# The denominators of a softmax, summed over the partitions from two exact 16-bit halves

## The chip, the cores and the metric

The kernel runs on one core of one Trainium2 chip. The metric is the time of one execution on the device in microseconds; of several executions the median is given. A profile is taken of one further execution. Engines are named as the profile names them: PE is TensorE's matmul, PEld its load of weights, DVE is VectorE, ACT is ScalarE, POOL is GpSimd, SP issues most DMAs.

## The reference

Two groups of tokens (256 of a context, 2048 of a sample grid) pass through two layers. Each layer normalizes its input, projects it, and mixes three branches: attention with 8 heads on 2 key-value heads of 64 columns, a short convolution, and pooling. The output projection adds the result to the input. What the change touches is the attention of the sample tokens, 2048 queries against 2048 + 256 keys:

```python
s = jnp.einsum('bqkgd,btkd->bkgqt', qblk, k).astype(jnp.float32) * scale
p = jax.nn.softmax(s, axis=-1)
return jnp.einsum('bkgqt,btkd->bqkgd', p.astype(v.dtype), v)
```

All inputs are 32-bit. The kernel keeps that precision by splitting numbers into a high and a low part and multiplying the parts.

## The kernel before

Each layer has two phases: one with the input projection and the other branches, and one with attention and the output projection (`phase_b`). The attention goes over four blocks of 512 queries, and in a block over the 8 heads (in the last block in another order, with head 3 last). The first block of a layer also holds the context's heads. A head has nine steps; a step does 256 keys:

- `qk` (L1191, L1192): TensorE makes the scores `st` of 256 keys x 512 queries, with keys on the partitions.
- `expo` (L1201, L1203): ScalarE takes the exponential twice, 32-bit as `P` and 16-bit as `ph`. GpSimd subtracts, `pl` = `P` - `ph` (helper `padd`, L181), also 16-bit. `ph` and `pl` are the two halves that TensorE multiplies with the values (`pv`, L1237 and L1244), three steps later. The `pl` of all nine steps are multiplied together behind the last `ph`.
- `zsum` (L1223, `Z`): VectorE sums `P` over the keys of three steps that share a partition, in three pieces, one piece in each of the next steps. GpSimd adds the tiles of the three groups of steps. The result is a tile `Z` of 128 x 512: for each query, 128 partial denominators.
- `max_pieces` (L1152, L1159, `mx`; L1153, L1161, `mr`): beside this, TensorE makes the scores of a later head once more, and VectorE takes their maximum. These `mx` tiles have two accumulators in PSUM, which rotate; other small groups, `lc` among them, take theirs from the same two.
- `outproj` (L1370 to L1372, `op`): the previous block's output projection, in small pieces between the steps.

The sum of `Z` over the partitions is `fin_b` (L1272, `lc`): for each of four groups of 128 queries, a matmul with the piece of `Z` as weights and a 128 x 2 tile of ones as the moving operand. VectorE takes the reciprocal `rl`. It is queued two steps after the step that issues the head's last `pv`, which is at the end of the next head's fifth step.

The last head of the last block is different: its `Z` isn't added, two tiles go into `lc`.

A manual schedule sets the order: each engine carries out its instructions in the order in which the code issues them, and semaphores hold an instruction back until what it reads is there and the buffer that it writes is free. Work is put into steps by tables (`todo`, `first`), and runs at the end or the start of its step.

The option that is changed was there before, switched off (`'fh': 0`).

Of the kernel before, what the change touches and what calls it, by code (L numbers as in the profile page):

```python
# [11 lines left out]
F16 = mybir.dt.float16  # L12
I32 = mybir.dt.int32
AF = mybir.ActivationFunctionType
ALU = mybir.AluOpType
# [16 lines left out]
PR = {'oa': 6, 'po': 4, 'q1': 3, 'q2': 5, 's0': 14, 's0p': 7, 'q1p': 2, 'ma': 3, 'mb': 1, 'd0': 3, 'd1': 2, 'dp': 1,  # L32
# [7 lines left out]
V_SCALE = 1.0  # L40

# [54 lines left out]
def hybrid_step(ctx: ExitStack, tc: tile.TileContext, A, O):  # L96
# [942 lines left out]
    def phase_b(l, xs_src, xp_src, xs_dst, xp_dst, nxt):  # L1039


        last = l == DEPTH - 1
        with ExitStack() as st, ExitStack() as left:
            def pool(name, bufs=1, side="right", to=st, **kw):
                return to.enter_context(tc.tile_pool(name=name, bufs=bufs, side=side, reuse_waits="tile", **kw))
# [44 lines left out]
            def make_unit(prompt, blk, h):  # L1090

                u = U()
                u.prompt, u.blk, u.h = prompt, blk, h
                u.t0 = blk * 512
                u.nst = 1 if prompt else 9
                u.KH, u.KL, u.V = kvs[prompt]
                u.g = h // 4
                u.pair = h // 2
                u.odd = h % 2
                u.last = prompt or u.odd  # L1100
                u.hi, u.lo = ((slice(64, 128), slice(0, 64)) if u.odd else (slice(0, 64), slice(64, 128)))
                u.fh = int(PR['fh'] and blk > 0)
                u.P, u.pp, u.low, u.z = {}, {}, [], []
                return u

# [152 lines left out]

            def split_z(u):
                z = u.z[0]  # L1260
                zh = wk.tile([128, 512], F16, tag="zh", name="zh", bufs=1)
                nc.scalar.copy(out=zh, in_=z)
                zl = wk.tile([128, 512], F16, tag="zl", name="zl", bufs=1)
                (padd if PR['ze'] else dsub)(zl, z, zh, ALU.subtract)
                u.z2 = (zh, zl)

            def fin_b(u, bc):
# [340 lines left out]
            def add_unit(prompt, blk, h, B):  # L1608
                u = make_unit(prompt, blk, h)
                u.B = B  # L1610
                u.S = len(steps)
                units.append(u)
                steps.extend((u, j) for j in range(u.nst))
# [36 lines left out]
            def do_pv(s):  # L1650
# [11 lines left out]
                if u.fh:  # L1662
                    at(s + d - min(PR['ds'], d - 1), lambda: split_z(u))
# [38 lines left out]
            wk = pool("b_wk")  # L1702
# [9 lines left out]
            for s in range(NSTEP + LAG + 16):  # L1712
# [44 lines left out]
                if cur:  # L1757
                    u, j = cur
# [64 lines left out]
```

## Time and profile before

| what | value |
|---|---|
| median of three executions | 3217.0 us (3216.62 to 3223.13) |
| profiled execution | 3230.8 us, span 3229.0 us |
| PE, PEld busy | 3077.7 us (95%), 2443.4 us (76%) |
| DVE, ACT, POOL busy | 2320.5 us (72%), 1833.1 us (57%), 2017.3 us (62%) |
| attention, blocks 2 to 4 of layer 1 | from about 994 to 1600 us |
| the same of layer 2 | from about 2563 to 3172 us |
| mean granted clock of TensorE | 0.982 |

The span goes from the first to the last instruction; the rest of the time lies around it. Matmuls are pipelined, and a record is longer than what it adds: the distance from one start to the next is what counts. The granted clock is a share of 2.4 GHz; 0.50 is the 1.2 GHz level.

### The profile page before, as it was taken

The page shows a single profiled execution, that of the slowest core. Times are in us where ns is not written, and L with a number is a line of the kernel's source. Part 1 is how long each engine was busy: PE and PEld are TensorE (multiplying, and loading weights), DVE is VectorE, ACT ScalarE, POOL GpSimd, SP SyncE. Part 2 cuts the span into 40 slices and gives each one's busy share as a digit, 9 for nine tenths or more (in the row PEclk, how much of TensorE's full clock was granted, in tenths as well). Part 3 has the DMA queues.
Part 4 walks back from the last instruction along what each step waited for, and adds up shares of the span by engine and source line. Part 5 has one row for each costly group of instructions (what it writes and reads, how often), then busy time and mean ns, then how long its engine had stood idle before and what let it go on. Part 6 is the DMA issues. An engine that isn't in the chain of part 4 may idle for free. (4 is left out here: it accounts for less than half of the span.)

```text
span 3229.0 us, 48081 instructions
## 1 busy us (share of the span) xinstructions
PE 3077.7 (95%) x17642; PEld 2443.4 (76%) x17642; DVE 2320.5 (72%) x3728; ACT 1833.1 (57%) x2634; POOL 2017.3 (62%) x1290
## 2 busy tenths in 40 slices
PE   7899999999999999999979899999999999999997
PEld 5788888776677777777769788987676777677775
DVE  5655576358888888888757545843778888888886
ACT  3323233237777777777742323331668887787785
POOL 2424363226888888888833334621578888898885
PEclk9999999999999999999989999999999999999999
DMA  7245744346233241323433455434623432242444
GB/s 248 75 143 164 241 158 149 118 130 167 77 120 113 68 125 58 105 79 110 137 127 100 152 160 193 132 98 120 175 66 119 130 97 80 86 131 86 131 144 149
DMA packets 371970, 408.40 MB, mean 126 GB/s; under 512 B 33428, under 2 KB 319640, under 8 KB 370968
## 3 DMA queue, kind: packets, MB, share of 16 engines
q1 hardware_dynamic: 371736, 405.33, 40.6%
q8 instruction: 140, 2.29, 0.3%
q14 instruction: 94, 0.77, 0.1%
HBM read 285.69 MB, written 119.55 MB: 126 GB/s over the span
## 5 line engine op out<-in xcount | busy, mean ns | idle before, releaser
L181 POOL TENSOR_TENSOR pl<-P,ph 128x1024 f16<-128x1024 f32 (+2 forms) x594 | 1235.7, 2091 | 282.7 <-ACT ph L1203 260.9
L1153 DVE TENSOR_REDUCE mr<-mx 128x1 f32<-128x512 f32 x1024 | 696.3, 685 | 276.8 <-PE mx L1152 270.8
L1201 ACT ACTIVATE P<-st 128x1024 f32<-128x1024 f32 x576 | 636.1, 1104 | 286.3 <-PE st L1192 281.2
L1223 DVE TENSOR_REDUCE Z<-P 128x152 f32<-128x912 f32 (+2 forms) x576 | 695.9, 1209 | 6.6 <-ACT P L1201 5.5
L1203 ACT ACTIVATE ph<-st 128x1024 f16<-128x1024 f32 x584 | 591.6, 1013 | 0.0
L1152 PE MATMUL mx<-KH,T 128*128 128x512 f32 x1024 | 485.4, 475 | 33.5 <-DVE mr L1153 16.7
L639 PE MATMUL rest<-xh,wh 128*128 128x512 f32 (+1 forms) x1264 | 477.8, 378 | 0.7 <-ACT wh L426 0.7
L641 PE MATMUL rest<-xh,wl 128*128 128x512 f32 (+1 forms) x1264 | 468.8, 371 | 2.0 <-DVE wl L428 2.0
L640 PE MATMUL rest<-xl,wh 128*128 128x512 f32 (+1 forms) x1264 | 469.2, 371 | 0.0
L1191 PE MATMUL st<-T,KH 128*128 128x512 f32 x1152 | 462.3, 401 | 3.1 <-ACT ph L1203 3.1
L1192 PE MATMUL st<-T,KL 65*128 65x512 f32 x1152 | 460.1, 399 | 0.0
L1237 PE MATMUL pv<-ph,V 128*128 128x512 f16 x1152 | 351.8, 387 | 2.2 <-ACT P L1201 1.8
L1152 PEld LDWEIGHTS mx<-KH,T 128*128 128x128 f32 x1024 | 194.2, 190 | 192.7 <-DVE mr L1153 83.0
L428 POOL TENSOR_TENSOR wl<-wf,wh 128x512 fp32r<-128x512 f32 x88 | 124.1, 1410 | 244.5 <-ACT wh L426 226.4
L639 PEld LDWEIGHTS rest<-xh,wh 128*128 128x128 f32 x1264 | 240.7, 190 | 44.4 <-issue 5.5
L641 PEld LDWEIGHTS rest<-xh,wl 128*128 128x128 f32 x1264 | 240.1, 190 | 43.8 <-DVE wl L428 2.6
L640 PEld LDWEIGHTS rest<-xl,wh 128*128 128x128 f32 x1264 | 240.6, 190 | 36.9
L1192 PEld LDWEIGHTS st<-T,KL 65*128 65x128 f32 x1152 | 219.2, 190 | 47.7
L1191 PEld LDWEIGHTS st<-T,KH 128*128 128x128 f32 x1152 | 220.0, 191 | 42.5 <-ACT ph L1203 6.1
L480 PE MATMUL qkv<-wl,xh 128*128 128x256 f32 x864 | 247.5, 287 | 4.7 <-DVE wl L428 3.1
L479 PE MATMUL qkv<-wh,xh 128*128 128x256 f32 x864 | 251.3, 291 | 0.0
L481 PE MATMUL qkv<-wh,xl 128*128 128x256 f32 x864 | 246.9, 286 | 0.0
(234 smaller groups left out, 5559.8 us busy)
## 6 DMA issues: line engine op xcount, KB each, us to landing
wo<-woH SPq DMA_DIRECT2D x144, 256.0 KB
wo<-woL SPq DMA_DIRECT2D x144, 256.0 KB
wf<-in_w_in SPq DMA_DIRECT2D x50, 512.0 KB
wa<-in_w_ada SPq DMA_DIRECT2D x24, 1024.0 KB
wf<-in_w_in SPq DMA_DIRECT2D x19, 1024.0 KB
woH<-wgh SPq DMA_DIRECT2D x64, 256.0 KB
woL<-wgl SPq DMA_DIRECT2D x64, 256.0 KB
T<-qH SPq DMA_DIRECT2D x128, 128.0 KB
```

Of the source, the lines that this page charges most:

```text
L181: nc.gpsimd.tensor_tensor(out=out, in0=a, in1=b, op=op)
L639: nc.tensor.matmul(out=ps[:, 0:b.n], lhsT=wh[:, k, ms], rhs=b.h[:, k, :], start=(k == 0), stop=False)
L640: nc.tensor.matmul(out=ps[:, 0:b.n], lhsT=wh[:, k, ms], rhs=b.l[:, k, :], start=False, stop=False)
L641: nc.tensor.matmul(out=ps[:, 0:b.n], lhsT=wl[:, k, ms], rhs=b.h[:, k, :], start=False, stop=(k == KD - 1))
L1152: nc.tensor.matmul(out=ps, lhsT=u.T1[:, q * 128:(q + 1) * 128], rhs=u.KH[u.g][:, c * 512:(c + 1) * 512])
L1153: nc.vector.reduce_max(out=mr[:, q, c:c + 1], in_=ps, axis=AX.X)
L1191: nc.tensor.matmul(out=ps[:, i, :], lhsT=u.KH[u.g][:, kt], rhs=u.T1, start=True, stop=False)
L1192: nc.tensor.matmul(out=ps[:, i, :], lhsT=u.KL[u.g][0:65, kt], rhs=u.T2, start=False, stop=True)
L1201: nc.scalar.activation(out=P, in_=ps, func=AF.Exp, scale=0.125)
L1203: nc.scalar.activation(out=ph, in_=ps, func=AF.Exp, scale=0.125)
L1223: nc.vector.tensor_reduce(out=z[:, c], in_=u.P[grp][:, 0:ns, c, :].rearrange("p s n t -> p n s t"), axis=AX.XY, op=ALU.add)
L1237: nc.tensor.matmul(out=u.po, lhsT=u.V[u.g][:, 2 * j + i, :], rhs=ph[:, i, :], start=(j == 0 and i == 0), stop=False)
```

## The change

For the heads of the second to fourth block (all but the last head of the last block), `split_z` makes two 16-bit tiles of `Z`: `zh`, the rounded value, and `zl` = `Z` - `zh`. Both lie in one tile `zhl`, which takes a buffer of the tag `Z` (three of 2 KB, as before). ScalarE makes `zh`; `zl` is GpSimd's in the first layer and VectorE's in the second. `lc` then takes eight 16-bit matmuls with 16-bit ones in place of four 32-bit ones, each of which is two passes in the trace. `split_z` is queued at the end of the step before `lc`.

```diff
-      'n2': 4, 'fh': 0, 'tpos': 0, 'ze': 0, 'ds': 1, 'zb': 3, 'dl': 2, 'm3': 1000, 'hk': 2, 'hc': 2,
+      'n2': 4, 'fh': 1, 'tpos': 0, 'ze': 0, 'ds': 1, 'zb': 3, 'dl': 2, 'm3': 1000, 'hk': 2, 'hc': 2,
...
-                u.fh = int(PR['fh'] and blk > 0)
+                u.fh = int(PR['fh'] and blk > 0 and not (blk == 3 and h == 3))
...
             def split_z(u):
                 z = u.z[0]
-                zh = wk.tile([128, 512], F16, tag="zh", name="zh", bufs=1)
+                two = wk.tile([128, 2, 512], F16, tag="Z", name="zhl", bufs=PR['zb'])
+                zh, zl = two[:, 0], two[:, 1]
                 nc.scalar.copy(out=zh, in_=z)
-                zl = wk.tile([128, 512], F16, tag="zl", name="zl", bufs=1)
-                (padd if PR['ze'] else dsub)(zl, z, zh, ALU.subtract)
+                (dsub if last else padd)(zl, z, zh, ALU.subtract)
                 u.z2 = (zh, zl)
```

TensorE, first layer, second block, at the fifth step of a head (`zhl` is the tile of both halves; what an instruction waits for stands in brackets). Before:

```order
L1192 MATMUL st<-T_9655,KL 128x512
L1191 MATMUL st<-T_9262,KH 128x512
L1192 MATMUL st<-T_9655,KL 128x512
L1159 MATMUL mx<-KH,T_9544 128x256 x2
L1272 MATMUL lc<-vones,Z 128x2 x4
```

With the change:

```order
L1159 MATMUL mx<-KH,T_10152 128x256 [waits DVE_49]
L1159 MATMUL mx<-KH,T_10152 128x256
L1272 LDWEIGHTS zhl [waits Activation_49]
L1272 MATMUL lc<-vones_h,zhl 128x2 [waits DVE_49]
L1272 LDWEIGHTS zhl [waits Pool_49]
L1272 MATMUL lc<-vones_h,zhl 128x2
```

The place is the same; six more pairs like the last follow. The second load, the first of `zl`, waits for GpSimd, where the old group waited for GpSimd's addition of `Z`.

GpSimd, first layer, around the same place, with the change (before, the row with `zhl` isn't there and nothing else differs):

```order
L181 TENSOR_TENSOR Z<-Z 128x512 [waits DVE_49,PE_49,Pool_49]
L181 TENSOR_TENSOR pl<-P,ph 128x1024 [waits PE_49,Activation_49]
L181 TENSOR_TENSOR pl<-P,ph 128x1024 [waits Activation_49]
L181 TENSOR_TENSOR zhl<-Z,zhl 128x512 [waits Activation_49]
L181 TENSOR_TENSOR pl<-P,ph 128x1024 [waits PE_49,Activation_49] x4
```

The subtraction stands behind the two `pl` that follow the addition of `Z`.

VectorE, second layer, with the change:

```order
L1153 TENSOR_REDUCE mr<-mx 128x1 [waits PE_49]
L184 TENSOR_TENSOR zhl<-Z,zhl 128x512 [waits Activation_49]
L1161 TENSOR_REDUCE mr<-mx 128x2 [waits PE_49]
L1223 TENSOR_REDUCE Z<-P 128x190
L1161 TENSOR_REDUCE mr<-mx 128x2 [waits PE_49]
L1275 RECIPROCAL rl<-lc 128x4 [waits PE_49]
```

The subtraction is new; the two `mr` behind it free the accumulators that `lc` and the next `mx` take.

## Rows read from the trace of the kernel before

**Rows 1.** The page, part 1: busy time, share of the span, instructions.

```profile
PE 3077.7 (95%) x17642; PEld 2443.4 (76%) x17642; DVE 2320.5 (72%) x3728; ACT 1833.1 (57%) x2634; POOL 2017.3 (62%) x1290
```

**Rows 2.** Windows: length; PE, PEld, DVE, ACT, POOL busy; clock, DMA share, GB/s.

```profile
994.00:1600.00 606.00, 598.54 (x3446) 454.44 (x3446) 509.53 (x707) 458.82 (x562) 508.57 (x270) 1.00 0.30 89
2563.00:3172.00 609.00, 598.96 (x3415) 450.90 (x3414) 509.04 (x710) 487.34 (x671) 534.14 (x323) 1.00 0.35 107
```

**Rows 3.** Groups by line and shape: busy us, mean ns of one, idle before.

```profile
L1272 PE MATMUL lc<-vones,Z 128*128 128x2 f32 x592 | 74.6, 248 | 5.1 <-DVE mr L1153 2.6 <-DVE mr L1161 1.4 <-POOL pl L181 0.2
L1272 PEld LDWEIGHTS lc<-vones,Z 128*128 128x128 f32 x592 | 73.1, 193 | 14.0 <-DVE mr L1153 5.3 <-issue 4.8 <-POOL pl L181 2.1
L1237 PEld LDWEIGHTS <-V 128*128 128x128 f16 x1152 | 68.2, 99 | 57.5 <-issue 35.6 <-PE mx L1152 2.5
...
L181 POOL TENSOR_TENSOR pl<-P,ph 128x512 f16<-128x512 f32 x18 | 21.2, 1179 | 0.0
L1304 ACT CAST mixh<-o 128x512 fp32r<-128x512 f32 x32 | 19.9, 621 | 22.8 <-POOL o L181 16.3 <-DVE o L184 6.4
...
L184 DVE TENSOR_TENSOR o<-o,zs 128x512 f32<-128x512 f32 x2 | 1.4, 692 | 0.1
```

**Rows 4.** Timeline of PE at one head: start, us, instruction, idle before.

```profile
1076.35 1.01 PE L1272 MATMUL lc<-vones,Z 128*128 128x2 f32 x8
```

**Rows 5.** Timeline of POOL at the same head.

```profile
1076.21 2.16 POOL L181 TENSOR_TENSOR pl<-P,ph 128x1024 f16<-128x1024 f32 x1
```

**Rows 6.** Timelines of PE and POOL at the first and the last of 22 heads.

```profile
994.04 0.24 PE L1272 MATMUL lc<-vones,Z 128*128 128x2 f32 x1 [0.19 <-DVE mr L1161]
994.81 2.16 POOL L181 TENSOR_TENSOR pl<-P,ph 128x1024 f16<-128x1024 f32 x1
...
1570.94 0.24 PE L1272 MATMUL lc<-vones,Z 128*128 128x2 f32 x1
1570.79 2.16 POOL L181 TENSOR_TENSOR pl<-P,ph 128x1024 f16<-128x1024 f32 x1
```

**Rows 7.** Timelines of DVE and POOL in the first layer's projection phase.

```profile
372.97 1.79 DVE L784 TENSOR_TENSOR wg<-wo,gate 128x512 f32<-128x512 f32 x1
372.93 1.29 POOL L428 TENSOR_TENSOR wl<-wf,wh 128x512 fp32r<-128x512 f32 x1 [0.60 <-ACT wh L426]
```

**Rows 8.** Timelines of ACT, POOL, DVE and PE at a head of the second layer.

```profile
2755.23 1.00 ACT L1203 ACTIVATE ph<-st 128x1024 f16<-128x1024 f32 x1
2755.27 2.16 POOL L181 TENSOR_TENSOR pl<-P,ph 128x1024 f16<-128x1024 f32 x1
2756.70 0.68 DVE L1161 TENSOR_REDUCE mr<-mx 128x2 f32<-128x512 f32 x1
2758.55 0.68 DVE L1161 TENSOR_REDUCE mr<-mx 128x2 f32<-128x512 f32 x1
2757.54 1.02 PE L1272 MATMUL lc<-vones,Z 128*128 128x2 f32 x8
2759.47 0.58 PE L1152 MATMUL mx<-KH,T 128*128 128x512 f32 x1
```

**Rows 9.** The same at a head with a late `ph`.

```profile
3119.38 0.99 ACT L1203 ACTIVATE ph<-st 128x1024 f16<-128x1024 f32 x1
3120.45 2.14 POOL L181 TENSOR_TENSOR pl<-P,ph 128x1024 f16<-128x1024 f32 x1 [0.49 <-ACT ph L1203]
3120.24 0.35 PE L1272 MATMUL lc<-vones,Z 128*128 128x2 f32 x2
```

**Rows 10.** Windows around two stops of PE, columns as in group 2.

```profile
472.84:475.77 2.93, 0.00 (x1) 0.00 (x1) 2.90 (x9) 1.29 (x3) 0.82 (x1) 0.88 0.01 3
475.10:481.90 6.80, 6.13 (x28) 6.13 (x29) 6.53 (x15) 0.00 (x0) 5.24 (x4) 0.50 0.39 117
2241.85:2244.13 2.28, 0.00 (x1) 0.03 (x1) 0.00 (x0) 0.00 (x0) 0.00 (x0) 1.00 1.10 241
2244.13:2251.00 6.87, 6.87 (x30) 5.56 (x31) 4.84 (x7) 0.60 (x1) 0.00 (x0) 1.00 1.11 216
```

## The prediction

> **What bounds the kernel now.** I read the page first, then the windows of the two attention stretches, then the timeline around one group of matmuls, engine by engine. The page says TensorE: busy 95% of the span, every other engine at most 72% [rows 1]. The windows of the three changed blocks say it more sharply [rows 2]: 598.54 of 606 us in the first layer and 598.96 of 609 us in the second. So in these stretches a microsecond that TensorE waits is a microsecond of the result, and one that it saves is saved, unless another engine then ends last. GpSimd is the next busiest, 508.57 and 534.14 us of them; most of that is `pl`, 2.16 us a step. VectorE has 509 us.
>
> The place that the change touches is the group `lc` at the end of the fifth step of the next head, once for each head. TensorE takes its instructions in order: what stands behind a late `lc` (the output projection, `pv`, the next `mx` and `st`) is late too, and ScalarE, VectorE and GpSimd wait for `st`.
>
> **The change, part by part.** 46 heads are changed: 23 of 24 in each layer.
>
> *Removed.* Today's `lc` group is eight passes over 32-bit weights: 1.01 us of records, each some 0.25 long, so starts 0.11 apart and 0.88 us of TensorE [rows 3, 4]. *Put in its place* are eight passes over 16-bit weights. No such small 16-bit pass is in the trace. Bounds: as dear as now (no gain), or nearly free (0.8 us saved). The nearest row is the 16-bit load of `V`, 99 ns of record against 193 for the load in `lc` [rows 3], about half; by it a pass takes about 0.055 and a group saves 0.45 us: 23 x 0.45 = 10 us in each layer. [...] I keep the row.
>
> *Added, ScalarE.* The copy `zh`, bounded by a cast of the same 128x512 size: 0.62 us [rows 3]. It stands behind `ph`, in time in which ScalarE waits for the next `st`, and costs nothing by itself. The tile is taken from the three buffers of `Z`; I find no reduce that waits longer for that, since what it takes over was read a step or more earlier.
>
> *Added, GpSimd, first layer.* The subtraction `zl`: 1.18 us by the `pl` of 128x512 [rows 3]. It stands on GpSimd's queue behind the addition of `Z` and two `pl`, and `lc` needs it one step later. Before, `lc` needed only that addition. In the head that I took as the example, `lc` starts at 1076.35 [rows 4], while the second of the two `pl` runs from 1076.21 for 2.16 us, to 1078.37 [rows 5]. `zl` is then done at 1079.55. The first pass (on `zh`) can run, the second load waits: it would have started at 1076.46, so TensorE stands for 3.1 us. The backlog doesn't come from a full queue that a shift would change: the addition of `Z` waits for a reduction on VectorE that follows the end of the head's `pv`, and both `pl` stand behind it. The same two rows for each head give `pl` ending after `lc` starts by 2.93 us in the first head [rows 6], 2.01 in the last of them, 1.3 to 3.8 in the 22 heads, on average 2.06; the 23rd has it done in time. The stall is thus 2.06 + 1.18 - 0.11 = 3.1 us, 22 x 3.1 = 69 us (hand-overs left out), less the 10 us of shorter passes: +59 us. Nothing gives it back: while TensorE stands, the others run dry and wait for the next `st`.
>
> *Added, VectorE, second layer.* There the subtraction is VectorE's, between the last `mr` of a step and the first of the next. Undisturbed it takes 0.69 us (a subtraction or product of 128x512 from SBUF: 692 ns [rows 3]). But both inputs lie in SBUF, and such an operation waits out a running GpSimd operation: a product of the same size took 1.79 us and ended 0.54 us after the GpSimd subtraction that ran beside it (372.97 + 1.79 = 374.76, and 372.93 + 1.29 = 374.22) [rows 7]. In the attention stretch GpSimd runs a `pl` most of the time. Example [rows 8]: `ph` ends at 2756.23, `zh` at 2756.85; a `pl` runs to 2757.43, so `zl` ends at about 2757.97 (not 2757.54). The first `mr` behind it then ends at 2758.65 instead of 2757.38, 1.27 us late. `lc` takes the accumulator that this `mr` frees, so it starts at 2758.65 instead of 2757.54; and the second `mr`, also 1.27 late (2760.50), holds the next `mx`, which stood at 2759.47: TensorE is 1.03 us late behind it, with the shorter passes already used up. In the worst heads `ph` itself is late: ending at 3120.37, with a `pl` from 3120.45 to 3122.59 [rows 9], `zl` ends at 3123.13, the `mr` at 3123.81, and `lc` at 3120.24 is 3.6 us late. The same arithmetic over the 22 heads before the last ones gives 0.4 to 3.5 us each, 36 us in all: +36 us. Without the wait for GpSimd it would be about 18 us; with it I have only the rows of another phase, so 18 to 36 is the bound, and I take 36 since `pl` reads and writes SBUF just as that subtraction did.
>
> *The clock.* A TensorE that stands some 3 us can lose its clock. It stood 2.93 us, and the next 6.80 us were granted 0.50, the 1.2 GHz level [rows 10]; it stood 2.28 us at another place and kept 1.00. 6.8 us at half clock cost 3.4 us of work. For the 22 stalls of the first layer that is 0 to 75 us. Theirs, some 2.9 us after the first pass, lie at the longer of the two, but two cases of another phase are few; I take one stall in four: +19 us.
>
> **Sum.** 59 + 36 + 19 = 114 us. The rows come from an execution of 3230.8 us (span 3229.0, 1.8 around it), which is 13.8 us (0.4%) over the median of 3217.0; the terms are differences, so I set them on the median: 3217 + 114 = 3331, say 3330 us.
>
> **The rivals.**
> - *The clock holds.* For it: the 2.28 us that cost nothing [rows 10]. Then 3217 + 59 + 36 = 3312.
> - *The clock falls after nearly every stall.* For it: the 2.93 us [rows 10]. 3217 + 95 + 75 = 3387. The Trainium skill's page "TensorE: Matmul & The Clock Gate", section "Why this matters for your kernels", speaks for this one: it warns of idle gaps between bursts of matmuls because the clock goes to half behind them.
> - *VectorE is hardly held by GpSimd, and passes are nearly free.* 3217 + 69 - 23 x 0.8 + 16 = 3284. For it: no row has these two instructions side by side.
> - *The subtraction is in time (the other side).* If GpSimd were as far as `lc` with its queue, the place of the wait would be empty, only the shorter passes would count, 46 x 0.45 = 21 us: 3196. It decides at `zl` ending before `lc` starts, that is GpSimd 3.1 us further than the rows have it [rows 4 to 6]. One head of 23 is that far. In the second layer, `zl` would have to leave the `mr` behind it on time, and 0.69 us alone doesn't.
> - *No change that shows.* The stalls would have to shrink to the 21 us saved; half of the first layer's alone is more.
>
> **How the numbers follow.** Stalls with some falls of the clock (3315 to 3370), the forecast: 0.45. Stalls without (3290 to 3315): 0.22. Clock falling nearly always (3370 to 3400): 0.09. Small waits (3255 to 3290): 0.15. In time: 0.05; no change: 0.04. The range 3270 to 3390 leaves out about 2 in 10. Its ends are worked from the bounds: below, 69 - 18 + 16 with a seventh off the stalls, and no fall of the clock; above, all 22 falls. Faster by over 0.2% (about what a measurement of this kernel can tell from no change): 0.05; within: 0.04; slower: 0.91.
>
> **What would show it.** In the first layer, `lc` waiting for GpSimd's `zl` some 3 us in 22 heads, and `zl` starting when the second `pl` ends, 1.2 us long. In the second, `zl` on VectorE taking 0.7 us where no `pl` runs and up to 2.3 where one does, `lc` waiting for VectorE's `mr`, a stretch of 609 us becoming about 645. 16-bit `lc` loads of about 0.1 us of record. The first layer's stretch of 606 us becoming 665 to 740. Wrong it is if `lc` waits under 1 us for `zl` in the first layer, if the `op` behind `lc` comes no later after the step's `st` than now, or if the granted clock of the first stretch falls well under 0.9.

## The result, and the profile after

The kernel with the change takes 3368.25 us (median), the kernel before 3216.81 on the same chip: the ratio is 1.0459 (95% interval 1.044 to 1.0479), so it is slower by some 148 to 151 us. Forecast were 3330 us in a range of 3270 to 3390, that is +113.

The first part of the page (busy time, share of the span, instructions) and the row of granted clocks, with the change:

```profile
PE 3102.8 (92%) x17642; PEld 2450.3 (73%) x17642; DVE 2366.0 (70%) x3751; ACT 1856.7 (55%) x2680; POOL 2051.2 (61%) x1313
...
PEclk9999999999999989989989999999999999999999
```

Against [rows 1] the matmuls are as many, but TensorE is busy 92% of the span where it was 95%, and 25 us longer in all, though the new passes are shorter: part of its work ran at a lower clock.

Windows from the first changed `lc` to the last in each layer, with the change (columns as in group 2):

```profile
991.94:1690.40 698.46, 624.63 (x3443) 470.24 (x3442) 513.49 (x707) 470.57 (x583) 531.43 (x292) 0.93 0.26 78
2650.80:3316.45 665.65, 610.57 (x3442) 453.21 (x3442) 550.03 (x735) 498.62 (x696) 545.02 (x327) 0.96 0.31 96
```

And the same stretches, between the same two instructions, of the kernel before:

```profile
994.04:1599.70 605.66, 598.24 (x3442) 454.11 (x3443) 509.19 (x707) 458.69 (x561) 508.38 (x270) 1.00 0.30 89
2563.92:3177.12 613.20, 602.74 (x3442) 454.57 (x3443) 511.45 (x713) 489.44 (x677) 538.34 (x328) 1.00 0.34 105
```

The first layer loses 92.8 us and the second 52.5. Together that is 145.3, a little more than the 139.2 between the two profiled executions (3369.97 and 3230.8 us). In both layers the granted clock is down. A mean of 0.93 over 698 us is some 98 us at 0.50 (0.07 x 698 / 0.5); 0.96 over 666 us is some 53.

What the new instructions cost (view of the tile `zhl` with the change; the three numbers are shortest, median and longest in ns):

```profile
L1272 PEld LDWEIGHTS <-zhl x368: 95/96/119, 991.7 to 3316.6; 128*128 128x128 f16 x184
L1272 PE MATMUL lc<-vones_h,zhl x368: 163/163/188, 991.9 to 3316.6; 128*128 128x2 f16 x184
L1263 ACT CAST zhl<-Z x46: 602/619/656, 990.8 to 3314.4; 128x512 f16<-128x512 f32 x46
L181 POOL TENSOR_TENSOR zhl<-Z,zhl x23: 1141/1151/1185, 994.9 to 1690.5; 128x512 f16<-128x512 f32 x23
L184 DVE TENSOR_TENSOR zhl<-Z,zhl x23: 794/1203/7153, 2648.4 to 3315.0; 128x512 f16<-128x512 f32 x23
```

And what TensorE waited for at `lc` (view of the tile `lc`: us, times):

```profile
  POOL zhl L181: 68.4, 23
  PE lc L1272: 44.4, 24
  DVE mr L1161: 37.3, 14
  DVE mr L1153: 7.9, 14
  ACT P L1201: 7.4, 8
```

The prices of ScalarE and GpSimd are those of [rows 3]. GpSimd's 23 subtractions hold TensorE for 68.4 us. In the second layer the same engine waits at `lc` for `mr` (37.3 us), and for ScalarE's `P` by the record (7.4); the 7.9 us of the other `mr` were there before (2.6 and 5.3 us in [rows 3]). The 44.4 us named "PE lc" are VectorE's `rl`, which waits for `lc`, not TensorE.

A head of the first layer with the change (timeline: start, us, engine, instruction, idle before):

```profile
1051.15 1.29 POOL L181 TENSOR_TENSOR Z<-Z 128x512 f32<-128x512 f32 x1 [0.35 <-DVE Z L1223]
1052.40 4.28 POOL L181 TENSOR_TENSOR pl<-P,ph 128x1024 f16<-128x1024 f32 x2
1056.62 1.17 POOL L181 TENSOR_TENSOR zhl<-Z,zhl 128x512 f16<-128x512 f32 x1
...
1053.53 0.61 ACT L1263 CAST zhl<-Z 128x512 f16<-128x512 f32 x1
...
1054.77 0.16 PE L1272 MATMUL lc<-vones_h,zhl 128*128 128x2 f16 x1
1057.85 0.35 PE L1272 MATMUL lc<-vones_h,zhl 128*128 128x2 f16 x7 [2.92 <-POOL zhl L181]
1058.05 0.56 PE L1370 MATMUL op<-wo,ch 128*128 128x256 f32 x1
1058.41 0.41 PE L1371 MATMUL op<-wo,ch 128*128 128x256 f32 x1
```

`zh` is done at 1054.14, before `lc` starts; the first pass runs at 1054.77. GpSimd still has a `pl` until 1056.68 and only then begins `zl`. TensorE stands for 2.92 us, and the `op` behind `lc` (L1371) takes 0.41 us where such a record takes 0.28 at full clock (below, at 2741.40). The clock around this stop, in windows:

```profile
1054.93:1057.85 2.92, 0.01 (x1) 0.01 (x1) 1.63 (x2) 1.70 (x2) 2.92 (x3) 0.85 0.99 297
1057.00:1063.80 6.80, 5.96 (x26) 4.93 (x27) 2.64 (x5) 1.07 (x2) 2.88 (x2) 0.50 0.34 90
```

The 6.80 us at 0.50, 1.2 GHz, begin 0.85 us before the stop ends; TensorE works for 5.96 us of them. In the trace 20 of the first layer's 22 stops have a fall to 0.50, which begins between 2.4 us before the stop's end and 1.1 us behind it.

Two heads of the second layer with the change, one with a short and one with a long subtraction:

```profile
2739.54 0.79 DVE L184 TENSOR_TENSOR zhl<-Z,zhl 128x512 f16<-128x512 f32 x1 [0.40 <-ACT zhl L1263]
2740.26 0.68 DVE L1161 TENSOR_REDUCE mr<-mx 128x2 f32<-128x512 f32 x1
...
2740.99 0.34 PE L1272 MATMUL lc<-vones_h,zhl 128*128 128x2 f16 x8 [0.94 <-ACT P L1201]
2741.19 0.37 PE L1370 MATMUL op<-wo,mixh 128*128 128x256 f32 x1
2741.40 0.28 PE L1371 MATMUL op<-wo,mixh 128*128 128x256 f32 x1
...
2742.84 0.50 PE L1152 MATMUL mx<-KH,T 128*128 128x512 f32 x1 [0.24 <-DVE mr L1161]
...
2947.07 2.15 POOL L181 TENSOR_TENSOR pl<-P,ph 128x1024 f16<-128x1024 f32 x1
2949.18 1.26 POOL L181 TENSOR_TENSOR oy<-oy,fg 128x512 f32<-128x512 f32 x1
2950.40 4.16 POOL L181 TENSOR_TENSOR pl<-P,ph 128x1024 f16<-128x1024 f32 x2
...
2947.96 7.15 DVE L184 TENSOR_TENSOR zhl<-Z,zhl 128x512 f16<-128x512 f32 x1 [0.38 <-ACT zhl L1263]
2955.03 0.68 DVE L1161 TENSOR_REDUCE mr<-mx 128x2 f32<-128x512 f32 x1
2955.77 0.35 PE L1272 MATMUL lc<-vones_h,zhl 128*128 128x2 f16 x8 [7.14 <-DVE mr L1161]
2956.34 0.41 PE L1371 MATMUL op<-wo,mixh 128*128 128x256 f32 x1
```

In the first head `lc` starts when the `mr` behind `zl` ends (2740.94), 0.94 us late; the record names ScalarE's `P` there, but VectorE's `mr` ends last. In the second head `zl` starts under a running `pl` and ends at 2955.11, 0.55 us after the fourth GpSimd instruction (2954.56). `lc` stands 7.14 us, and the `op` behind it runs at half clock (0.41 us). The row of eight passes also prices a pass: (0.34 - 0.16) / 7 = 26 ns apart, where the 32-bit ones were 0.11 us apart; the `op` starts 0.20 us after the group. A group saves 0.88 - 0.21 = 0.67 us, 15 us in each layer.

### The profile page after: what moved, and what is told of

Its sections match the earlier page's. It is cut to its first block, busy times and chain, and to the rows that moved or that the text cites. A ratio compares the mean times of both kernels' runs of the same rounds, so it can differ in the third digit from the quotient of the medians.

```text
span 3368.2 us, 48107 instructions
## 1 busy us (share of the span) xinstructions
PE 3102.8 (92%) x17642; PEld 2450.3 (73%) x17642; DVE 2366.0 (70%) x3751; ACT 1856.7 (55%) x2680; POOL 2051.2 (61%) x1313
## 4 chain that ended last, share of the span: by engine, by line
PE 57%; DVE 15%; POOL 6%; issue 4%; ACT 4%; DMA 3%; SPq 1%; POOLq 0%; DVEq 0%; ACTq 0%
PE mx L1152 6%; PE rest L639 5%; PE rest L640 5%; PE rest L641 5%; PE pv L1237 5%; PE st L1191 5%; PE st L1192 5%; DVE Z L1223 4%; DVE mr L1153 4%; PE pv L1244 4%; POOL pl L181 3%; PE op L1370 2%; PE op L1371 2%; PE op L1372 2%; PE qkv L480 1%
## 5 line engine op out<-in xcount | busy, mean ns | idle before, releaser
L1152 PE MATMUL mx<-KH,T 128*128 128x512 f32 x1024 | 499.6, 489 | 35.4 <-DVE mr L1153 16.8
L1191 PE MATMUL st<-T,KH 128*128 128x512 f32 x1152 | 473.3, 411 | 3.3 <-ACT ph L1203 3.3
L1192 PE MATMUL st<-T,KL 65*128 65x512 f32 x1152 | 469.4, 407 | 0.0
L1237 PE MATMUL pv<-ph,V 128*128 128x512 f16 x1152 | 364.7, 400 | 2.2 <-ACT P L1201 1.8
L1152 PEld LDWEIGHTS mx<-KH,T 128*128 128x128 f32 x1024 | 201.4, 197 | 204.9 <-DVE mr L1153 82.9
L639 PEld LDWEIGHTS rest<-xh,wh 128*128 128x128 f32 x1264 | 240.8, 191 | 44.4 <-issue 5.5
L1192 PEld LDWEIGHTS st<-T,KL 65*128 65x128 f32 x1152 | 226.0, 196 | 50.4
L1191 PEld LDWEIGHTS st<-T,KH 128*128 128x128 f32 x1152 | 227.6, 198 | 45.8 <-ACT ph L1203 6.8
```

The lines of the kernel that those rows point to most:

```text
L639: nc.tensor.matmul(out=ps[:, 0:b.n], lhsT=wh[:, k, ms], rhs=b.h[:, k, :], start=(k == 0), stop=False)
L1152: nc.tensor.matmul(out=ps, lhsT=u.T1[:, q * 128:(q + 1) * 128], rhs=u.KH[u.g][:, c * 512:(c + 1) * 512])
L1191: nc.tensor.matmul(out=ps[:, i, :], lhsT=u.KH[u.g][:, kt], rhs=u.T1, start=True, stop=False)
L1192: nc.tensor.matmul(out=ps[:, i, :], lhsT=u.KL[u.g][0:65, kt], rhs=u.T2, start=False, stop=True)
L1237: nc.tensor.matmul(out=u.po, lhsT=u.V[u.g][:, 2 * j + i, :], rhs=ph[:, i, :], start=(j == 0 and i == 0), stop=False)
```

## The experiments

All edits are to the changed kernel; the stretches are those of the windows above, first layer / second layer (before: 605.7 / 613.2 us; with the change 698.5 / 665.7). A ratio is to the kernel before on the same chip: 3226.36 us for experiments 1 to 4, 3222.98 for 5 to 8, 3220.26 for 9 to 12. The expected times are set on 3217 us, so a few microseconds between them and a measured time say little. A stretch is of one execution.

**1. The first layer alone.** Does each layer carry its own loss?

```diff
-                u.fh = int(PR['fh'] and blk > 0 and not (blk == 3 and h == 3))
+                u.fh = int(PR['fh'] and blk > 0 and not last and not (blk == 3 and h == 3))
```

> The split in the first layer alone. If the two layers lose apart from each other, this run keeps the first layer's loss of the changed kernel (its stretch from the first to the last changed lc is 698 us against 606, so +93) and gives back the second's (666 against 613, +52): about 3310 us. If what is lost in the first layer is partly regained later, less than 3300.

Measured: 3310.12 us, ratio 1.0259 (1.0244 to 1.0274); stretches 697.7 / 612.8. The layers are independent: the first keeps all its loss, the second has none.

**2. `lc` without the low half.** `zl` is still made, on the same engines in the same place, but nothing reads it: `lc` takes `zh` twice, so its passes are as many.

```diff
-                u.z2 = (zh, zl)
+                u.z2 = (zh, zh)
```

> zl is made by the same engines at the same places, but lc takes zh twice, so the low half is left out of the sum. Theory of the wait: in the first layer nothing reads zl, TensorE's 68 us of waiting and the clock's falls go, and the shorter passes gain some 15 us: its stretch is about 590 us. In the second layer lc is held by the mr behind zl on VectorE and not by zl, so its stretch stays near 660. Total about 3217 - 15 + 50 = 3250. Rival, the added work itself (GpSimd's and ScalarE's queues longer): the first stretch stays over 650 and the total over 3300. If in the second layer too it is the wait for zl itself that counts, total about 3190.

Measured: 3265.51 us, ratio 1.0127 (1.0108 to 1.0145). Its windows:

```profile
986.14:1585.46 599.32, 588.70 (x3443) 438.06 (x3442) 508.67 (x707) 470.39 (x583) 532.51 (x292) 1.00 0.30 91
2545.38:3210.82 665.44, 610.51 (x3443) 453.02 (x3442) 550.00 (x735) 498.77 (x696) 544.82 (x327) 0.96 0.31 96
```

In the first layer the whole loss is gone, and the clock is 1.00 again, though the stretch gains 6 us and not the 15 that the shorter passes were to bring: the loss was TensorE's wait for `zl` with what hangs on it; the copy, the subtraction and the shared buffer of `Z` cost nothing there. The second layer stays as it was, to 0.2 us: there `lc` isn't late by its own operand, but by the `mr` that stands behind `zl` on VectorE.

**3. The clock kept up.** 22 matmuls of 256 columns whose result nobody reads run ahead of each first-layer `lc`, in its wait. What the first layer regains is the clock's share, as far as the added matmuls fit into the wait.

```diff
-                ps = pmx.tile([128, 4, 2], F32, tag="mx", name="lc")
+                full = pmx.tile([128, 512], F32, tag="mx", name="lc")
+                ps = full[:, 0:8].rearrange("p (q e) -> p q e", e=2)
+                for _ in range(22 if u.fh and not last else 0):
+                    nc.tensor.matmul(out=full[:, 256:512], lhsT=ones_r, rhs=u.KH[u.g][:, 0:256])
```

> As the changed kernel, but in the first layer 22 matmuls of 256 columns that nobody reads stand ahead of each lc group, some 2.6 us of the 3.0 us that TensorE waits there. If the clock's falls cost what the half-clock stretches of the first layer say (20 falls, 99 us at half, so 40 to 49 us), the clock stays at 1.00 and the time falls to 3325 to 3335 although TensorE has more to do. Rival, the falls cost nothing beside the waits: 3365 to 3375.

Measured: 3332.53 us, ratio 1.0322 (1.0305 to 1.034). Its first window:

```profile
980.39:1643.52 663.13, 645.80 (x3927) 499.64 (x3928) 511.32 (x707) 470.14 (x583) 533.91 (x293) 1.00 0.27 82
```

With 484 matmuls more the stretch is 35.3 us shorter than 698.46, at a clock of 1.00. So some 35 us of the first layer's 93 are the clock, and 57 the waits less the shorter passes. (TensorE's busy time says the same: 624.63 with the change, 588.70 in experiment 2, a difference of 35.9.) The ratios put what the added matmuls give back higher, 1.0459 to 1.0322, 44 us with 36 to 53 as its interval; either way it is some two fifths to half of the layer's loss.

**4 and 5. The other engine.** The subtraction on VectorE in both layers, or on GpSimd in both.

```diff
-                (dsub if last else padd)(zl, z, zh, ALU.subtract)
+                dsub(zl, z, zh, ALU.subtract)
```

> The subtraction on VectorE in both layers. If VectorE's way costs in the first layer what it costs in the second (+52 rather than +93): about 3325. If GpSimd's queue is not what makes zl late, no change from 3368. If VectorE's waiting for GpSimd's pl is worse in the first layer: over 3368.

```diff
-                (dsub if last else padd)(zl, z, zh, ALU.subtract)
+                padd(zl, z, zh, ALU.subtract)
```

> The changed kernel with GpSimd subtracting in both layers, lc where it is. If the second layer's queue of GpSimd stands at lc as the first's does (the second pl ends 2.0 us behind the start of lc in most heads there too), its loss becomes that of the first, 90 to 100 rather than 52: about 3410. If VectorE is the worse place, under 3368.

Measured: on VectorE 3306.21 us, ratio 1.0248 (1.0223 to 1.0273), stretches 641.7 / 670.6; on GpSimd 3415.66 us, ratio 1.0598 (1.0569 to 1.0627), stretches 702.2 / 716.8. VectorE's way costs +36 us in the first layer (less than the 52 expected), GpSimd's +104 in the second. The two mechanisms belong to the engines, not to the layers. What TensorE waits for at `lc` with GpSimd in both:

```profile
  POOL zhl L181: 142.2, 45
```

That is 3.2 us each, where the first layer with the change has 3.0.

**6 to 8. `lc` two steps later.** Then GpSimd has the time it lacks. First the division of the change, then GpSimd in both layers, then a control without the split.

```diff
-                d = PR['dp'] if u.prompt else PR['dl'] if u is units[-1] else PR['d1' if u.blk else 'd0']
+                d = PR['dp'] if u.prompt else PR['dl'] if u is units[-1] else PR['d1' if u.blk else 'd0'] + 2 * (u.blk > 0)
...
-                    at(s + d - min(PR['ds'], d - 1), lambda: split_z(u))
+                    at(s + d - min(PR['ds'] + 2, d - 1), lambda: split_z(u))
```

> lc and all that follows from it two steps (some 5.3 us) later, the split where it is; GpSimd subtracts in the first layer, VectorE in the second. Theory of the wait: zl is 3.1 us late, so two steps later it is there, the first layer loses nothing and gains its 15 us. In the second layer VectorE still stands for GpSimd's pl ahead of two mr, but lc is no longer near: a part of the 52 us stays, 15 to 40. Total 3217 - 15 + 25 = 3227, 3215 to 3245. Rival, the engines' added work: 3300 or more.

The second has `padd(zl, ...)` of experiment 5 besides:

> The same with GpSimd subtracting in both layers, so VectorE gets no new work. Theory of the wait: both layers lose nothing and gain 0.65 us in each of 46 heads, 30 us: 3187, 3185 to 3205, faster than before. Rival, GpSimd at 88% of these stretches becomes the bound with 1.15 us more a head: over 3230.

The control has only the first line of the edit, and `'fh': 0`:

> The kernel before with lc two steps later and no split: the control of the two others. lc waited for little before, so the move alone gives nothing: 3217, 3205 to 3225. If the move alone gains as much as the run with GpSimd in both layers, the 16-bit passes gain nothing.

Measured: 3264.18 us, ratio 1.0124 (1.0099 to 1.015), stretches 607.2 / 653.9; 3221.87 us, ratio 0.9999 (0.9987 to 1.0011), stretches 607.2 / 618.4; control 3242.33 us, ratio 1.0057 (1.0038 to 1.0076), stretches 621.2 / 620.3. With time for `zl` the first layer's loss goes; VectorE's wait in the second doesn't, since it hangs on the `mr`, not on `lc`. All three came out slower than expected. The control shows one reason for the first two: the later `lc` itself costs 0.6%, where nothing was expected. A line of its waits of TensorE's loads (us, times, longest):

```profile
PEld op L1370 <- DVE ox L1374: 22.6, 18, 2.1
```

An `op` now waits 22.6 us for VectorE's `ox` before its loads. Against this control the split with GpSimd is some 19 us better (1.0057 to 0.9999), 14 of them in the first layer's stretch and 2 in the second's. So here a good part of the 30 us that the shorter passes save does show, but the two edits together give back only what the move takes.

**9 to 12. One step.** GpSimd in both layers, with `lc` one step later and the split in its place (9), the split one step earlier and `lc` in its place (10), both (11), and the later `lc` without a split (12).

```diff
-                d = PR['dp'] if u.prompt else PR['dl'] if u is units[-1] else PR['d1' if u.blk else 'd0']
+                d = PR['dp'] if u.prompt else PR['dl'] if u is units[-1] else PR['d1' if u.blk else 'd0'] + (u.blk > 0)
...
-                    at(s + d - min(PR['ds'], d - 1), lambda: split_z(u))
+                    at(s + d - min(PR['ds'] + 1, d - 1), lambda: split_z(u))
```

> lc and what follows one step (some 2.65 us) later, the split where it is, GpSimd subtracting in both layers. Theory of the wait: of the 3.0 us some 0.4 stay in each head, about as much as the shorter pass gives back (0.65): 0 to -10 us against before, and the move by one step should cost less than the 19 us that two steps cost. 3205 to 3225. If a move by one step costs like one by two, 3225 to 3240.

Number 10 has the old first line and `min(PR['ds'] + 1, d)`:

> lc in its old place, the split one step earlier, GpSimd subtracting in both layers: zl is done 2.1 us sooner, so 0.9 of the 3.0 us of waiting stay, a stop too short for the clock to fall; the shorter pass gives 0.65 back: +0.3 us in each of 46 heads, 3225 to 3240. If the clock falls even so, 3260 or more.

Number 11 has the new first line and `min(PR['ds'] + 2, d)`:

> As the run with one step, and the split one step earlier, so zl stands ahead of the second pl on GpSimd's queue and is done 2.1 us sooner: nothing is left of the wait at lc, only ScalarE's copy now stands ahead of a P and waits there for GpSimd's addition of Z (about 1 us). 3195 to 3215. If ScalarE's delay reaches st, 3220 to 3240.

Number 12 has the new first line and `'fh': 0`:

> The kernel before with lc one step later and no split: the control of the two runs with one step. 3217 to 3240 (two steps cost 19 us); what the split is worth is the difference to this one.

Measured: (9) 3238.55 us, ratio 1.0058 (1.0045 to 1.0072); (10) 3251.81 us, 1.0104 (1.0087 to 1.0122); (11) 3219.66 us, 0.9999 (0.9987 to 1.0012); (12) 3220.48 us, 1.0001 (0.9991 to 1.0011). The stretches are 612.0 / 631.2, 618.7 / 626.7, 607.0 / 614.4 and 607.5 / 610.2. In 9 `lc` still waits 36.9 us for `zl`, in 10 it waits 28.7; both missed what was expected, by 10 us and more, and not all of that is explained by these waits. In 11 no wait for `zl` is left, and yet it gains nothing on its control 12; it was expected 5 us faster at least. Some waits of TensorE's loads and of ScalarE in 11 (us, times, longest):

```profile
PEld mx L1152 <- DVE mr L1153: 94.2, 160, 2.6
...
PEld mx L1159 <- DVE mr L1153: 16.2, 21, 1.9
...
ACT zhl L1263 <- POOL Z L181: 62.0, 46, 2.2
```

And in 12:

```profile
PEld mx L1152 <- DVE mr L1153: 71.4, 122, 2.5
```

The windows of the second layer, first 11, then 12, show the saving as shorter busy time of TensorE, 593.37 us against 600.87, in a stretch that is no shorter (so it is idle for 21.0 us against 9.3):

```profile
2560.91:3175.27 614.36, 593.37 (x3441) 437.59 (x3440) 513.19 (x710) 500.61 (x699) 560.85 (x349) 0.99 0.34 104
```

```profile
2552.63:3162.79 610.16, 600.87 (x3440) 455.10 (x3441) 511.54 (x710) 492.80 (x677) 536.92 (x327) 0.99 0.35 106
```

So in 11 the time that the passes save comes back as waits. Which waits is not shown. TensorE's loads wait some 23 us longer for VectorE's maxima (`mr`), but loads run beside matmuls, so not all of that is lost. ScalarE's copy now stands ahead of a `P` and waits 62.0 us for GpSimd's addition of `Z`, 1.3 us a head; the expectation had named this as what could eat the gain, and no run parts the two.

No version tried is measurably faster than the kernel before.

## Why the prediction was right, and where its sizes were off

**The wait in the first layer: right, to a microsecond.** 22 stalls of 3.1 us, 69 us, were forecast; measured are 68.4 in 23 (the 23rd, which was to be in time, waits 1.1). `zl` starts when the second `pl` ends, and takes 1.15 us, as [rows 3 to 6] gave it. With the clock kept up (experiment 3) the layer loses 57 us against the 59 of the sum.

**The clock: right in kind, the term too small.** I took one stall in four, 19 us. Experiment 3 measures some 35 us in the first layer by the stretch (44 by the ratios), where 20 of 22 stops have a fall. Of the two stops of [rows 10] the one of 2.93 us was the like case. The bound of 75 us was too high by its own row: the 6.80 us at 0.50 begin 0.67 us before TensorE starts again (475.10 against 475.77), which then works 6.13 us and loses 3.1 us of work at most, not 3.4; that makes 67. Measured is about half: the rival "the clock falls after nearly every stall" was right about the falls and wrong in the price of one. 22 falls as long as that of the row would be 150 us at 0.50; the window has some 98, and TensorE works in some 87 of them, so that they cost 44 at most. The warning of the Trainium skill, "TensorE: Matmul & The Clock Gate", section "Why this matters for your kernels", holds here: the head shown has its 0.41 us matmuls right behind a gap of 2.92 us.

**The second layer: right in its mechanism, 16 us short.** That `zl` waits out GpSimd, and that `mr` carries the delay to `lc` and the next `mx`, is shown by experiment 2 (nothing changes when `lc` doesn't need `zl`) and by the rows of 2739 and 2947. The Trainium skill, "SBUF — State Buffer", section "SBUF: two separate sides", says that a VectorE instruction with two inputs in SBUF and a GpSimd instruction that reads SBUF exclude each other for a whole instruction; the rows agree in 21 of 23 heads, in which `zl` is held by one GpSimd instruction at most. The step of the sum that was missing is the clock: I had no term for it in this layer, though the stalls there were to last up to 3.6 us. TensorE's busy time is 610.57 us, against 593.37 in experiment 11 with the same instructions on TensorE: about 17 us, an estimate that no run isolated. (The layer's stretch has 51 us at 0.50, and TensorE works in some 44 of them, which bounds it at 22.) The two heads in which `zl` waited longer than forecast (7.15 and 4.01 us, where up to 2.3 was expected) add to it, and the shorter passes take from it; how these divide stays open. (The lower price of VectorE's way is 18 us where it is worked out and 16 in the rival and the range; that changes nothing.)

**The shorter passes: right in sign, too small.** 26 ns and not 55: 0.67 us a group, not 0.45. The load's record did halve, from 192 to 96 ns, as the row of `V` had it; what failed is the step from the record to the distance between passes, which fell from 110 ns to 26. The Trainium skill, "TensorE: Matmul & The Clock Gate", section "Weight-path perf modes", gives about twice as fast, as measured, for a load of 128 columns that isn't 32-bit: the record agrees, the distance doesn't follow it. How much of the saving reaches the time depends on what else waits: experiment 2 shows 6 us of the first layer's 15, experiment 7 some 19 of 30 against its control, experiment 11 none.

**What cost nothing.** ScalarE's copy and the buffer of `Z`: right (experiment 2).

**The rivals.** "The clock holds" falls by the windows; "small waits" and "in time" by 68.4 us at `lc`; "no change" by the interval. "In time" was made true in experiment 11, by other moves than the change's, and there its 21 us didn't come; in experiment 7 about as much came, and the move of `lc` took it.

So the error of 35 to 38 us is mainly the clock: some 16 us short in the first layer by experiment 3 (shown, more by the ratios) and about as much in the second (an estimate), with a few microseconds of the other terms.

## What to carry to other kernels

Before work is handed to an engine that has spare time on average, read where that engine stands in its queue at the moment the result is needed: here the new instruction took 1.2 us, and its place behind two others made it 3. Where the receiver is the busiest engine, add to each stop what it runs slower behind it. And a saving on the busiest engine need not reach the time when it works in a loop with others: with the stall taken away, one schedule here kept some 19 of 30 us that the 16-bit passes had saved, and another none.

## What the runs showed that I had not expected

- A 16-bit load with a matmul of two columns behind it repeats every 26 ns, against 110 ns a pass with 32-bit weights [rows 4], though the record of the load is only halved (96 against 192 ns).
- A VectorE subtraction from SBUF was held over four GpSimd instructions in a row (7.15 us) in one head and over two (4.01 us) in another, though in 21 heads it got in behind the first.
- Short waits left little time at half clock: 28.7 us in 44 waits over both layers (experiment 10) left 14 and 10 us at 0.50 in the two stretches, where 68.4 us in 23 waits left some 98 in the first alone.
